# A 16x512x1024 by 1024x768 product with a subtraction: smaller row groups, a pinned order, and a transpose of f16 pairs as 32-bit words

## The chip, the cores and the metric

The kernel runs on one core of one Trainium2 chip. The metric is the device time in microseconds (us) of one execution; three runs of the kernel before gave 228.85, 230.29 and 231.27 us.

## The reference

```python
def setup_inputs():
    batch, m, k, n = 16, 512, 1024, 768
    return {
        "x": np.random.randn(batch, m, k).astype(np.float32),
        "weight": np.random.randn(k, n).astype(np.float32),
        "sub_value": np.random.randn(batch, m, n).astype(np.float32),
    }

def reference(x, weight, sub_value):
    return (np.matmul(x, weight) - sub_value).astype(np.float32)
```

Flattened, x is 8192 rows of 1024, and out and sub_value are 8192 rows of 768, all f32.

## The kernel before

The 8192 rows of x are cut into 64 "m tiles" of 128 rows. Four m tiles make a group (`SUP = 4`), and one DMA moves a whole group of x (2 MB), of sub_value or of out (1.5 MB each), with four neighbouring rows of memory on one partition. There are 16 groups.

Each m tile goes through five steps. ScalarE casts its x rows from f32 to f16 (L104, `do_cast`). TensorE transposes the 128x1024 f16 tile in eight blocks of 128x128, each a weight load of the x block and a matmul with the f16 identity (L112, `do_transpose`), into one PSUM tile. ScalarE copies the transposed tile to SBUF (L117, `xt_tile`). TensorE then multiplies: for the output columns 0 to 511 and again for 512 to 767 it runs over the eight k tiles (L127, `do_matmul`), so 8 matmuls of 512 columns and 8 of 256, each with its own weight load of an `xt_tile` block. VectorE subtracts sub_value from PSUM into `out_tile` (L136), and after the fourth m tile one DMA stores the group (L143).

The weight is read at the start in eight pieces of 128 k rows (L88) through a staging pool of two buffers, and VectorE casts each piece to f16 (L89). All DMAs are issued by SyncE (SP) on one queue. A scheduler orders the instructions of each engine; the source is written with casts 9 m tiles ahead and transposes 6 m tiles ahead of the matmuls (`C_AHEAD`, `T_AHEAD`), and the pools hold 4 x groups, 3 sub groups, 2 out groups, 8 `xt_tile`, 4 PSUM tiles for transposes and 2 for products.

Of the kernel before, what the change touches and what calls it, by code (L numbers as in the profile page):

```python
# [1 line left out]

# [5 lines left out]

P = 128
F32 = mybir.dt.float32  # L10
F16 = mybir.dt.float16


@with_exitstack
def kernel(
    ctx: ExitStack,
    tc: tile.TileContext,
    x: bass.AP,
    weight: bass.AP,
    sub_value: bass.AP,  # L20
    out: bass.AP,
):
    nc = tc.nc

    x_flat = x.flatten_outer_dims()
    sub_flat = sub_value.flatten_outer_dims()
    out_flat = out.flatten_outer_dims()

    M_TOT, K = x_flat.shape
    _, N = weight.shape  # L30
    assert M_TOT % P == 0
    assert K % P == 0
    n_mtiles = M_TOT // P
    n_ktiles = K // P

    SUP = 4
    assert n_mtiles % SUP == 0
    n_sup = n_mtiles // SUP

    x_sup_ap = x_flat.rearrange("(s p j) k -> s p j k", p=P, j=SUP)  # L40
    sub_sup_ap = sub_flat.rearrange("(s p j) n -> s p j n", p=P, j=SUP)
    out_sup_ap = out_flat.rearrange("(s p j) n -> s p j n", p=P, j=SUP)

    n_splits = []
    n0 = 0
    while n0 < N:
        w = min(512, N - n0)
        n_splits.append((n0, w))
        n0 += w

    T_AHEAD = 6
    C_AHEAD = 9
    X_AHEAD = 3

    const_pool = ctx.enter_context(tc.tile_pool(name="const", bufs=1))
    w_stage_pool = ctx.enter_context(tc.tile_pool(name="w_stage", bufs=2))
    w_pool = ctx.enter_context(tc.tile_pool(name="w_pool", bufs=1))
    x_pool = ctx.enter_context(tc.tile_pool(name="x_pool", bufs=X_AHEAD + 1))
    x16_pool = ctx.enter_context(tc.tile_pool(name="x16_pool", bufs=6))
    xt_pool = ctx.enter_context(tc.tile_pool(name="xt_pool", bufs=T_AHEAD + 2))  # L60
    sub_pool = ctx.enter_context(tc.tile_pool(name="sub_pool", bufs=3))
    out_pool = ctx.enter_context(tc.tile_pool(name="out_pool", bufs=2))
    psum_t_pool = ctx.enter_context(tc.tile_pool(name="psum_t", bufs=4, space=bass.MemoryType.PSUM))
    psum_o_pool = ctx.enter_context(tc.tile_pool(name="psum_o", bufs=2, space=bass.MemoryType.PSUM))

    identity = const_pool.tile([P, P], F16)
    make_identity(nc, identity)

    w_sb = w_pool.tile([P, n_ktiles, N], F16)

    x_tiles: dict[int, bass.AP] = {}

    def load_x_sup(s):
        t = x_pool.tile([P, SUP, K], F32, tag="x", name="x_tile")
        x_tiles[s] = t
        nc.sync.dma_start(out=t, in_=x_sup_ap[s])  # L76

    sub_tiles: dict[int, bass.AP] = {}

    def load_sub_sup(s):  # L80
        t = sub_pool.tile([P, SUP, N], F32, tag="sub", name="sub_tile")
        sub_tiles[s] = t
        nc.sync.dma_start(out=t, in_=sub_sup_ap[s])

    load_x_sup(0)
    for kt in range(n_ktiles):
        w_stage = w_stage_pool.tile([P, N], F32, name="w_stage")
        nc.sync.dma_start(out=w_stage, in_=weight[kt * P : (kt + 1) * P, :])  # L88
        nc.vector.tensor_copy(out=w_sb[:, kt], in_=w_stage)  # L89
    for s in range(1, X_AHEAD + 1):  # L90
        if s < n_sup:
            load_x_sup(s)
    load_sub_sup(0)
    if n_sup > 1:
        load_sub_sup(1)

    x16_tiles: dict[int, bass.AP] = {}
    xt_tiles: dict[int, bass.AP] = {}

    def do_cast(mi):  # L100
        s, j = divmod(mi, SUP)
        t = x16_pool.tile([P, K], F16, name="x16_tile")
        x16_tiles[mi] = t
        nc.scalar.copy(out=t, in_=x_tiles[s][:, j])  # L104

    def do_transpose(mi):
        x16_tile = x16_tiles.pop(mi)
        xt_tile = xt_pool.tile([P, n_ktiles, P], F16, name="xt_tile")
        xt_tiles[mi] = xt_tile
        psum_t = psum_t_pool.tile([P, n_ktiles, P], F16, name="psum_t")  # L110
        for kt in range(n_ktiles):
            nc.tensor.transpose(  # L112
                psum_t[:, kt, :],
                x16_tile[:, kt * P : (kt + 1) * P],
                identity,
            )
        nc.scalar.copy(out=xt_tile, in_=psum_t)  # L117

    out_tiles: dict[int, bass.AP] = {}

    def do_matmul(mi):
        s, j = divmod(mi, SUP)
        xt_tile = xt_tiles.pop(mi)
        psum_o = psum_o_pool.tile([P, N], F32, name="psum_o")
        for n0, nw in n_splits:
            for kt in range(n_ktiles):
                nc.tensor.matmul(  # L127
                    psum_o[:, n0 : n0 + nw],
                    xt_tile[:, kt, :],
                    w_sb[:, kt, n0 : n0 + nw],  # L130
                    start=(kt == 0),
                    stop=(kt == n_ktiles - 1),
                )
        if j == 0:
            out_tiles[s] = out_pool.tile([P, SUP, N], F32, name="out_tile")
        nc.vector.tensor_tensor(  # L136
            out=out_tiles[s][:, j],
            in0=psum_o,
            in1=sub_tiles[s][:, j],
            op=mybir.AluOpType.subtract,  # L140
        )
        if j == SUP - 1:
            nc.sync.dma_start(out=out_sup_ap[s], in_=out_tiles.pop(s))  # L143

    for mi in range(min(C_AHEAD, n_mtiles)):
        do_cast(mi)
    for mi in range(min(T_AHEAD, n_mtiles)):
        do_transpose(mi)

    for mi in range(n_mtiles):  # L150
        s, j = divmod(mi, SUP)
        if j == 0:
            if s + X_AHEAD + 1 < n_sup:
                load_x_sup(s + X_AHEAD + 1)
            if s + 2 < n_sup:
                load_sub_sup(s + 2)
        if mi + C_AHEAD < n_mtiles:
            do_cast(mi + C_AHEAD)
        if mi + T_AHEAD < n_mtiles:
            do_transpose(mi + T_AHEAD)  # L160
        do_matmul(mi)


# [1 line left out]
_INS = ['x', 'weight', 'sub_value']  # L165
_OUTS = [((16, 512, 768), 'float32')]


# [23 lines left out]
```

## Time and profile before

| what | value |
|---|---|
| median of the runs | 230.29 us (228.85 to 231.27) |
| profiled execution: its span, first to last instruction (the page gives no other time of it) | 229.0 us |
| TensorE matmul busy | 203.4 us, 89% |
| TensorE weight load busy | 132.6 us, 58% |
| ScalarE busy | 124.0 us, 54% |
| VectorE busy | 65.8 us, 29% |
| moved by DMA | 87.26 MB, mean 381 GB/s |
| granted TensorE clock, mean | 0.961 |

Busy time is the sum of the recorded durations on an engine; TensorE overlaps neighbouring matmuls, so a recorded duration (219 ns for a transpose) is longer than the distance from one start to the next. The median of the timed runs lies 1.3 us above the profiled span.

### The profile page before, as it was taken

The numbers are of one execution on the slowest core, as the hardware profiler recorded it, in microseconds if no ns is written. First come the engines' busy times: TensorE is split into PE (matmuls) and PEld (weight loads), VectorE is DVE, ScalarE is ACT, GpSimd is POOL, SyncE is SP. The second block draws the span as 40 slices with busy tenths as digits, with TensorE's granted clock in tenths as the row PEclk, the third lists the DMA queues.
The fourth block names the chain that finished last, engine by engine and source line by source line (L and its number), as shares of the span: only waits on it lengthen the run. The fifth ranks groups of instructions, "written<-read, shape, count | busy, mean of one in ns | idle before, by whom it ended". The sixth has DMA issues, their size and how long they took to land.

```text
span 229.0 us, 3465 instructions
## 1 busy us (share of the span) xinstructions
PE 203.4 (89%) x1536; PEld 132.6 (58%) x1536; DVE 65.8 (29%) x72; ACT 124.0 (54%) x129; POOL 0.7 (0%) x6
## 2 busy tenths in 40 slices
PE   0259559999999999999999999999999999999970
PEld 0236325666666676666757576667575766666540
DVE  0101113333333331423332413333332413233430
ACT  2499863382583666566583939475656565510000
POOL 1000000000000000000000000000000000000000
PEclk9995967999999999999999999999999999999996
DMA  6999999999999999999999999999999999750606
GB/s 235 421 429 401 427 431 432 419 399 412 352 427 427 439 419 433 425 436 420 430 429 431 423 424 426 431 426 423 429 423 435 424 416 350 305 240 39 271 6 275
DMA packets 8079, 87.26 MB, mean 381 GB/s; under 512 B 896, under 2 KB 896, under 8 KB 1920
## 3 DMA queue, kind: packets, MB, share of 16 engines
q1 hardware_dynamic: 8064, 87.04, 91.1%
q8 instruction: 12, 0.20, 0.3%
q14 instruction: 3, 0.02, 0.0%
HBM read 61.87 MB, written 25.17 MB: 380 GB/s over the span
## 4 chain that ended last, share of the span: by engine, by line
PE 82%; DMA 12%; DVE 1%; ACT 0%; SPq 0%; issue 0%
PE psum_o L127 72%; DMA w_stage<-in_weight_dram 12%; PE psum_t L112 10%; DVE w_sb L89 1%; ACT xt_tile L117 0%; DVE out_tile L136 0%; SPq L88 0%; SPq L76 0%
## 5 line engine op out<-in xcount | busy, mean ns | idle before, releaser
L127 PE MATMUL psum_o<-w_sb,xt_tile 128*128 128x512 f16 (+1 forms) x1024 | 174.7, 330 | 3.6 <-DVE w_sb L89 3.1
L127 PEld LDWEIGHTS <-xt_tile 128*128 128x128 f16 x1024 | 100.1, 99 | 70.3 <-issue 4.6
L117 ACT COPY xt_tile<-psum_t 128x1024 f16<-128x1024 f16 x64 | 63.2, 1016 | 68.9 <-PE psum_t L112 37.6
L136 DVE TENSOR_TENSOR out_tile<-psum_o,sub_tile 128x768 f32<-128x768 f32 x64 | 61.3, 958 | 129.4 <-PE psum_o L127 126.2
L104 ACT CAST x_tile<-x_tile 128x1024 f16<-128x1024 f32 x64 | 63.5, 1053 | 8.8 <-DMA x_tile<-in_x_dram 8.8
L112 PE MATMUL psum_t<-identity,x_tile 128*128 128x128 f16 x512 | 37.4, 230 | 15.1 <-ACT x_tile L104 14.6
L112 PEld LDWEIGHTS <-x_tile 128*128 128x128 f16 x512 | 33.7, 104 | 19.0 <-ACT x_tile L104 16.1
L89 DVE CAST w_sb<-w_stage 128x768 f16<-128x768 f32 x8 | 4.5, 560 | 27.9 <-DMA w_stage<-in_weight_dram 27.9
L104 ACT ACT_TABLE_LOAD x1 | 1.3, 1283 | 0.7 <-PEq L176 0.7
masks.py:199 POOL TENSOR_SCALAR_AFFINE_SELECT identity<-identity 128x128 f16<-128x128 f16 x1 | 0.3, 294 | 0.1
masks.py:197 POOL MEMSET identity<- 128x128 f16 x1 | 0.2, 205 | 0.3 <-POOLq L176 0.3
L176 POOL MEMSET const-bfloat16-1.0<- 128x1 bf16 x1 | 0.1, 102 | 0.0
L176 POOL MEMSET const-uint8-127<- 128x1 uint8 x1 | 0.1, 102 | 0.0
L176 POOL MEMSET const-float32-0.0<- 128x1 f32 x1 | 0.1, 99 | 0.2 <-issue 0.2
L176 POOL MEMSET const-float32-1.0<- 128x1 f32 x1 | 0.1, 99 | 0.0
## 6 DMA issues: line engine op xcount, KB each, us to landing
x_tile<-in_x_dram SPq DMA_DIRECT2D x16, 2048.0 KB, 14.6
sub_tile<-in_sub_value_dram SPq DMA_DIRECT2D x16, 1536.0 KB, 17.8
out_dram<-out_tile SPq DMA_DIRECT2D x16, 1536.0 KB, 10.1
w_stage<-in_weight_dram SPq DMA_DIRECT2D x8, 384.0 KB, 6.3
```

The lines of the kernel that those rows point to most:

```text
L89: nc.vector.tensor_copy(out=w_sb[:, kt], in_=w_stage)
L104: nc.scalar.copy(out=t, in_=x_tiles[s][:, j])
L112: nc.tensor.transpose(psum_t[:, kt, :], x16_tile[:, kt * P : (kt + 1) * P], identity,)
L117: nc.scalar.copy(out=xt_tile, in_=psum_t)
L127: nc.tensor.matmul(psum_o[:, n0 : n0 + nw], xt_tile[:, kt, :], w_sb[:, kt, n0 : n0 + nw], start=(kt == 0), stop=(kt == n_ktiles - 1),)
L136: nc.vector.tensor_tensor(out=out_tiles[s][:, j], in0=psum_o, in1=sub_tiles[s][:, j], op=mybir.AluOpType.subtract,)
L176: nc = _bacc.Bacc("TRN2", target_bir_lowering=False, num_devices=1)
```

## The change

The kernel is rewritten around the same arithmetic in f16 with f32 accumulation.

- Groups are of two m tiles (`J = 2`), 32 of them. x moves in DMAs of 1 MB, sub_value and out in DMAs of 0.75 MB. The first x group is loaded in two halves.
- The weight comes in four pieces of 256 k rows (L73), each with a staging buffer of its own. In a piece, partition p holds the rows 2p and 2p+1, so the k index is split as (piece c, partition p, parity r).
- The f16 x tile is viewed as 128x512 words of 32 bits, each holding two neighbouring k. TensorE transposes four blocks of 128x128 words (L110) with an f32 identity. In the transposed tile the two k of a word stay side by side, so the stationary operand of a matmul (L127, L129) is taken with a step of two f16.
- The output is halved in 2 x 384 columns, one PSUM bank each, in place of 512 and 256; the product tiles in PSUM are three, the transpose tiles two.
- The result is written over the loaded sub_value tile (L142, `so_tile`), and the store (L89) goes out of it. There are 11 such tiles.
- Every instruction is kept in program order. TensorE issues a transpose of the m tile two ahead (`TA`) after every four matmuls; the cast runs four m tiles ahead. SP issues at the start of group g the load of x group g+4, of sub group g+2, and then the store of group g-2, and the last two stores behind the loop.

```diff
+J = 2
+D = 6
+TA = 2
+CA = 2
...
-    x_pool = ctx.enter_context(tc.tile_pool(name="x_pool", bufs=X_AHEAD + 1))
-    x16_pool = ctx.enter_context(tc.tile_pool(name="x16_pool", bufs=6))
-    xt_pool = ctx.enter_context(tc.tile_pool(name="xt_pool", bufs=T_AHEAD + 2))
-    sub_pool = ctx.enter_context(tc.tile_pool(name="sub_pool", bufs=3))
-    out_pool = ctx.enter_context(tc.tile_pool(name="out_pool", bufs=2))
-    psum_t_pool = ctx.enter_context(tc.tile_pool(name="psum_t", bufs=4, space=bass.MemoryType.PSUM))
-    psum_o_pool = ctx.enter_context(tc.tile_pool(name="psum_o", bufs=2, space=bass.MemoryType.PSUM))
-
-    identity = const_pool.tile([P, P], F16)
-    make_identity(nc, identity)
...
+    w_stage_pool = ctx.enter_context(tc.tile_pool(name="w_stage", bufs=n_c))
+    w_pool = ctx.enter_context(tc.tile_pool(name="w_pool", bufs=1))
+    x_pool = ctx.enter_context(tc.tile_pool(name="x_pool", bufs=6))
+    x16_pool = ctx.enter_context(tc.tile_pool(name="x16_pool", bufs=4))
+    xt_pool = ctx.enter_context(tc.tile_pool(name="xt_pool", bufs=4))
+    so_pool = ctx.enter_context(tc.tile_pool(name="so_pool", bufs=11))
+    psum_t_pool = ctx.enter_context(tc.tile_pool(name="psum_t", bufs=2, space=bass.MemoryType.PSUM))
+    psum_o_pool = ctx.enter_context(tc.tile_pool(name="psum_o", bufs=3, space=bass.MemoryType.PSUM))
+
+    ident = const_pool.tile([P, P], F32)
+    make_identity(nc, ident)
...
+    def load_w(c):
+        st = w_stage_pool.tile([P, 2, N], F32, name="w_stage")
+        keep(nc.sync.dma_start(out=st, in_=w_c[c]))
+        keep(nc.vector.tensor_copy(out=w_sb[:, c], in_=st))
...
+        def one(c):
+            def f():
+                if c == 0:
+                    start()
+                keep(nc.tensor.transpose(
+                    ps_t[mi].bitcast(F32)[:, c * P : (c + 1) * P],
+                    x16_t[mi].bitcast(F32)[:, c * P : (c + 1) * P],
+                    ident,
+                ))
+                if c == n_c - 1:
+                    fin()
+            return f
...
+                c, r = divmod(kt, 2)
+                lhsT = xt_t[mi][:, 2 * P * c + r : 2 * P * (c + 1) : 2]
+                for h in range(2):
+                    keep(nc.tensor.matmul(
+                        po_t[mi][:, h, :NS],
+                        lhsT,
+                        w_sb[:, c, r, h * NS : (h + 1) * NS],
+                        start=(kt == 0),
+                        stop=(kt == n_kt - 1),
+                    ))
...
+    load_x(0, 0)
+    load_w(0)
+    load_x(0, 1)
+    for c in range(1, n_c):
+        load_w(c)
+    load_x(1)
+    load_x(2)
+    load_sub(0)
+    load_x(3)
+    load_sub(1)
...
+        if g + 4 < n_g:
+            load_x(g + 4)
+        if g + 2 < n_g:
+            load_sub(g + 2)
+        if g - (D - 4) >= 0:
+            store(g - (D - 4))
...
+        for kt in range(n_kt):
+            mm[kt]()
+            if tr and kt % per == per - 1:
+                tr.pop(0)()
+        if mi + CA + TA < n_mt:
+            cast(mi + CA + TA)
+        finish(mi)
+    for g in range(n_g - (D - 4), n_g):
+        store(g)
```

In the middle of the program TensorE's row before passes from the last product of one m tile to a batch of transposes, each with a weight load row of its own (the names are those of the tiles; `x_tile` is the cast f16 tile here):

```order
L127 LDWEIGHTS xt_tile
L127 MATMUL psum_o<-w_sb,xt_tile 128x256
L112 LDWEIGHTS x_tile
L112 MATMUL psum_t<-identity,x_tile 128x128
L112 LDWEIGHTS x_tile
L112 MATMUL psum_t<-identity,x_tile 128x128
```

At the same place of the program after, a transpose stands alone between the products:

```order
L129 LDWEIGHTS xt_tile
L129 MATMUL psum_o<-w_sb,xt_tile 128x384
L110 MATMUL psum_t<-ident,x_tile 128x128
L129 LDWEIGHTS xt_tile
L129 MATMUL psum_o<-w_sb,xt_tile 128x384
```

What moved: the transposes are no longer in batches but one behind every four products, and the transpose of 32-bit words has no weight load row of its own; the one instruction loads its words itself.

SP's row at the start of the program before puts whole x groups between the pieces of the weight:

```order
L76 DMA x_tile<-in_x_dram 128x4096
L88 DMA w_stage<-in_weight_dram 128x768 x2
L76 DMA x_tile<-in_x_dram 128x4096
L88 DMA w_stage<-in_weight_dram 128x768 x2
L76 DMA x_tile<-in_x_dram 128x4096
L88 DMA w_stage<-in_weight_dram 128x768 x2
L76 DMA x_tile<-in_x_dram 128x4096
L88 DMA w_stage<-in_weight_dram 128x768 x2
L83 DMA sub_tile<-in_sub_value_dram 128x3072 x2
```

And after:

```order
L82 DMA x_tile<-in_x_dram 128x1024
L73 DMA w_stage<-in_weight_dram 128x1536
L82 DMA x_tile<-in_x_dram 128x1024
L73 DMA w_stage<-in_weight_dram 128x1536 x3
L80 DMA x_tile<-in_x_dram 128x2048 x2
L86 DMA so_tile<-in_sub_value_dram 128x1536
L80 DMA x_tile<-in_x_dram 128x2048
L86 DMA so_tile<-in_sub_value_dram 128x1536
```

What moved: one x group of two m tiles and the whole weight, 4.2 MB, now stand ahead of everything else in the queue, where 8 MB of x stood before the last pieces of the weight.

More of the change, by code (lines that the diff above doesn't have):

```diff
@@ L23 @@
     nc = tc.nc
+    keep = tc.keep_in_program_order
     x_flat = x.flatten_outer_dims()
@@ L30 @@
     _, N = weight.shape
[L31 to L49, printed above, removed]
@@ L64 @@
-    psum_o_pool = ctx.enter_context(tc.tile_pool(name="psum_o", bufs=2, space=bass.MemoryType.PSUM))
-    identity = const_pool.tile([P, P], F16)
-    make_identity(nc, identity)
[L69 to L101, printed above, removed]
-        t = x16_pool.tile([P, K], F16, name="x16_tile")
-        x16_tiles[mi] = t
-        nc.scalar.copy(out=t, in_=x_tiles[s][:, j])
@@ L106, in do_transpose @@
[L106 to L161, printed above, removed]
+    x_pool = ctx.enter_context(tc.tile_pool(name="x_pool", bufs=6))
@@ new lines @@
+    x16_pool = ctx.enter_context(tc.tile_pool(name="x16_pool", bufs=4))
[5 more added lines that the diff above has]
+    make_identity(nc, ident)
+    w_sb = w_pool.tile([P, n_c, 2, N], F16)
@@ new lines, with load_x @@
+    x_t = {}
+    so_t = {}
+    x16_t = {}
+    xt_t = {}
+    ps_t = {}
+    po_t = {}
+    def load_w(c):
+        st = w_stage_pool.tile([P, 2, N], F32, name="w_stage")
+        keep(nc.sync.dma_start(out=st, in_=w_c[c]))
+        keep(nc.vector.tensor_copy(out=w_sb[:, c], in_=st))
+    def load_x(g, js=None):
+        if g not in x_t:
+            x_t[g] = x_pool.tile([P, J, K], F32, name="x_tile")
+        if js is None:
+            keep(nc.sync.dma_start(out=x_t[g], in_=x_g[g]))
+        else:
+            keep(nc.sync.dma_start(out=x_t[g][:, js], in_=x_g[g][:, js]))
@@ new lines, in load_sub, with store, cast, transposes @@
+    def load_sub(g):
+        so_t[g] = so_pool.tile([P, J, N], F32, name="so_tile")
+        keep(nc.sync.dma_start(out=so_t[g], in_=sub_g[g]))
+    def store(g):
+        keep(nc.sync.dma_start(out=out_g[g], in_=so_t.pop(g)))
+    def cast(mi):
+        g, j = divmod(mi, J)
+        t = x16_pool.tile([P, K], F16, name="x16_tile")
+        x16_t[mi] = t
+        keep(nc.scalar.copy(out=t, in_=x_t[g][:, j]))
+    def transposes(mi):
+        def start():
+            ps_t[mi] = psum_t_pool.tile([P, K], F16, name="psum_t")
+        def fin():
+            xt = xt_pool.tile([P, K], F16, name="xt_tile")
+            xt_t[mi] = xt
+            keep(nc.scalar.copy(out=xt, in_=ps_t.pop(mi)))
+            x16_t.pop(mi)
+        def one(c):
[10 more added lines that the diff above has]
+            return f
+        return [one(c) for c in range(n_c)]
@@ new lines, in matmuls, with one, f @@
+    def matmuls(mi):
+        def one(kt):
+            def f():
+                if kt == 0:
+                    po_t[mi] = psum_o_pool.tile([P, 2, 512], F32, name="psum_o")
+                c, r = divmod(kt, 2)
[8 more added lines that the diff above has]
+                    ))
+            return f
+        return [one(kt) for kt in range(n_kt)]
@@ new lines, in finish, with transfers @@
+    def finish(mi):
+        g, j = divmod(mi, J)
+        o = so_t[g][:, j].rearrange("p (h n) -> p h n", h=2)
+        keep(nc.vector.tensor_tensor(
+            out=o, in0=po_t.pop(mi)[:, :, :NS], in1=o, op=mybir.AluOpType.subtract
+        ))
+    load_x(0, 0)
[8 more added lines that the diff above has]
+    load_sub(1)
+    def transfers(g):
+        if g + 4 < n_g:
[4 more added lines that the diff above has]
+            store(g - (D - 4))
@@ new lines @@
+    for mi in range(TA):
+        cast(mi)
+        for f in transposes(mi):
+            f()
+    for mi in range(TA, CA + TA):
+        cast(mi)
+    for mi in range(n_mt):
+        if mi % J == 0:
+            transfers(mi // J)
+        mm = matmuls(mi)
+        tr = transposes(mi + TA) if mi + TA < n_mt else []
+        per = max(1, n_kt // len(tr)) if tr else 1
+        for kt in range(n_kt):
[5 more added lines that the diff above has]
+        finish(mi)
```

13 lines of the change are left out of this document (9 added, 4 removed).

## The prediction

> **What bounds the kernel now.** I read the page first, for who is busy when, then the chain that ended last in order of time, then the windows for the rate of the transfers.
>
> ```profile
> span 229.0 us, 3465 instructions
> ...
> PE 82%; DMA 12%; DVE 1%; ACT 0%; SPq 0%; issue 0%
> ```
>
> The chain is TensorE for 82% of the span and a transfer for 12%. In order of time it shows where each of the two stands:
>
> ```profile
> 1.64 9.14 DMA w_stage<-in_weight_dram
> ...
> 25.13 6.69 DMA w_stage<-in_weight_dram
> ...
> 54.20 0.45 PE psum_t L112 x8
> 54.64 2.60 PE psum_o L127 x16
> ...
> 194.34 1.79 PE psum_t L112 x32
> 196.13 26.02 PE psum_o L127 x160
> ...
> 222.17 0.96 DVE out_tile L136
> ```
>
> Until 31.8 us the chain runs through the weight's pieces; from 32.5 us on it is TensorE without a hole. One m tile costs 0.45 us for eight transposes (0.45/8 = 56 ns each) and 2.60 us for sixteen matmuls (162 ns on average). That is 3.05 us, and 64 x 3.05 = 195 us. Now the transfers, in three stretches:
>
> ```profile
> core 0: us, PE busy (x) PEld busy (x) DVE busy (x) ACT busy (x) POOL busy (x), PEclk, DMA share, GB/s
> 0.00:5.00 5.00, 0.00 (x0) 0.00 (x0) 0.00 (x0) 1.28 (x1) 0.70 (x6) 1.00 0.64 206
> 5.00:185.00 180.00, 166.28 (x1286) 109.56 (x1287) 52.35 (x58) 113.07 (x118) 0.00 (x0) 0.96 1.01 423
> 185.00:229.00 44.00, 37.13 (x252) 23.02 (x249) 13.41 (x14) 9.66 (x10) 0.00 (x0) 0.95 0.57 231
> 10.00:30.00 20.00, 13.23 (x108) 9.29 (x109) 3.21 (x6) 18.10 (x20) 0.00 (x0) 0.83 1.01 419
> ...
> DMA packets 8079, 87.26 MB, mean 381 GB/s; under 512 B 896, under 2 KB 896, under 8 KB 1920
> ```
>
> From 5 to 185 us the DMA engines are full (share 1.01) at 423 GB/s. So **two resources are full at once**: TensorE needs 195 us and starts 32 us late, the transfers need 87.26 MB / 423 GB/s = 206 us and start at once. TensorE ends last only because of its late start. In the last 44 us the transfers run at half rate.
>
> **The change part by part.** First the *floor by transfers*, which no edit lowers: the bytes stay. The first 5 us moved 1.03 MB, worth 2.4 us at 423 GB/s, so the queue loses 2.6 us at the start. 2.6 + 206.3 = 208.9 us. The end costs a little more, as the answers for the store's line and for SP's waits show:
>
> ```profile
> L143 SPq DMA_DIRECT2D out_dram<-out_tile x16: 332/344/348, 44.8 to 223.2; - x16
> ...
> DMA to landing us min/median/max: 5.0/10.1/12.6
> ```
>
> ```profile
> SPq L187 <- DMA out_dram<-out_tile: 4.4, 1, 4.4
> ```
>
> The quickest store took 5.0 us for 1.57 MB, which at 423 GB/s is 3.7 us; 1.3 us is latency, part of it hidden in a full queue. The last store was issued at 223.2 us and, with SP's last wait of 4.4 us behind its issue of 0.3, landed at about 228; the span ended at 229.0, some 0.8 us later. I take 1.5 us for both: 210.4. Smaller pieces (8 and 6 KB per partition instead of 16 and 12) could cost something: the stretch from 10 to 30 us carried the weight in rows of 3 KB between the x groups and still ran at 419, 1% under 423. So between 0 and 1.5% of 206, or 0 to 3 us; I take 1. **Floor 211.5 us.**
>
> Does the queue stay full? SP keeps several transfers ahead; with the order of group g (x of g+4, sub of g+2, store of g-2), a store waits for a group that TensorE left a whole group ago, and behind it stand only loads that are needed three or four groups later. The last five stores follow the last sub load; each group of them is finished while the ones before are being written, so TensorE's end stays ahead of the queue if TensorE is the faster one.
>
> Second, *TensorE's own time*. Its start: x group 0 (1.05 MB), the weight (3.15) and x group 1 (1.05) are 5.24 MB. That is 2.6 + 5.24/0.423 = 15.0, with a microsecond to land 16 us. The pinned order needs group 1 before the fifth matmul, since the first transpose of m tile 2 stands there; its cast takes a microsecond more by the row below, so TensorE passes that point at 17.1 us, not at 32.5. In front of it lies only work that fits beside the loading.
>
> ```profile
> L127 PE MATMUL psum_o<-w_sb,xt_tile 128*128 128x512 f16 x512 | 124.1, 383 | 3.6 <-DVE w_sb L89 3.1 <-ACT xt_tile L117 0.3
> L127 PEld LDWEIGHTS <-xt_tile 128*128 128x128 f16 x1024 | 100.1, 99 | 70.3 <-issue 4.6 <-ACT xt_tile L117 1.1
> L127 PE MATMUL psum_o<-w_sb,xt_tile 128*128 128x256 f16 x512 | 68.1, 277 | 0.0
> L104 ACT CAST x_tile<-x_tile 128x1024 f16<-128x1024 f32 x64 | 63.5, 1053 | 8.8 <-DMA x_tile<-in_x_dram 8.8
> L117 ACT COPY xt_tile<-psum_t 128x1024 f16<-128x1024 f16 x64 | 63.2, 1016 | 68.9 <-PE psum_t L112 37.6 <-PE psum_o L127 30.9
> L136 DVE TENSOR_TENSOR out_tile<-psum_o,sub_tile 128x768 f32<-128x768 f32 x64 | 61.3, 958 | 129.4 <-PE psum_o L127 126.2 <-DMA sub_tile<-in_sub_value_dram 3.2
> L112 PE MATMUL psum_t<-identity,x_tile 128*128 128x128 f16 x512 | 37.4, 230 | 15.1 <-ACT x_tile L104 14.6 <-ACT xt_tile L117 0.5
> L112 PEld LDWEIGHTS <-x_tile 128*128 128x128 f16 x512 | 33.7, 104 | 19.0 <-ACT x_tile L104 16.1 <-issue 1.7
> ```
>
> Sixteen matmuls of 384 columns stream the same 6144 columns as eight of 512 and eight of 256, so 2.60 us again. A weight load of 99 ns lies beside a matmul of 162 ns. Its step of two f16 is not in the trace; a load would have to grow by 63 ns before it shows, so I take 0, and 63 ns beyond that as the upper end would cost 64 x 16 x 63 ns = 65 us of TensorE, a case that I count among the slow ones below.
>
> The transposes: eight of 56 ns go, four of t come. The trace has no transpose of 32-bit words. From below t is 56 ns, a transpose of the same 128 columns. From above, the nearest rows give 56 + 99 = 155 ns if the words' load, which is now inside the instruction, isn't hidden by the matmul before; 4 x 56 = 224 ns if a word of four bytes passes in four trips; and 323 ns for both. I take 56 to 90: the same count of columns and rows moves, and four matmuls stand ahead of each transpose to hide its load.
>
> Sum of TensorE: 17.1, the rest of m tile 0 at 12 x 0.162 = 1.95, 63 m tiles x 2.60 = 163.8, 248 transposes at t, then the subtraction 0.96, the store's issue 0.3, 0.79 MB / 423 GB/s = 1.9, its latency 1.3 and the end 0.8: **188.1 us + 248 t**. At t = 56 ns that is 202, under the floor. It meets the floor of 211.5 at t = 94 ns, and the span of before, 229.0, at t = 165 ns. So four transposes of up to 94 ns are free, and every further 10 ns cost 2.5 us.
>
> ScalarE keeps 1.05 + 1.02 = 2.07 us per m tile and VectorE 0.96, both under the 206.3/64 = 3.2 us that the transfers leave per m tile. TensorE will then wait about a tenth of the time; from 10 to 30 us it was busy for two thirds and the granted clock fell to 0.83, while at full work it stands at 1.00 or close by. Waits of a few tenths of a us between m tiles I cost at nothing, since a slower clock would fill them first. The in-place subtraction reads and writes as much as before, at the same 958 ns: 0. The store of a group holds its tile longer, but eleven tiles are a lead of nine groups. Four casts of the weight, each twice 560 ns, lie beside the loading.
>
> Span 211.5 us; the median of the runs stood 1.3 us over the profiled span of before, so I forecast **213 us** for the median, against 230.3.
>
> Two rules of the Trainium skill bear on t. Its page "TensorE: Matmul & The Clock Gate", section "Weight-path perf modes — Fast Weight Load (FWL) and DoubleRow", says that the fast weight load is on for 128 weights only where the type isn't f32. No run shown has an f32 load, so the trace can't say; by the page's P/1.2 = 107 ns for a plain load, an estimate, and no overlap, t would be 56 + 107 = 163 ns and the span 228.5. The same page's table of terms gives the transpose mode as four times faster for f32, which by an estimate would leave one trip in place of four, t = 56 ns and the floor. The page's section "Part 4: PE-mode transpose" has about 275 ns for a transpose in a kernel; this trace's rows disagree, 8 in 0.45 us.
>
> **The rivals.**
>
> *The words' load shows.* The order gives no weight load row for the new transpose; nothing in the trace says whether the engine still loads early. If it all shows, t = 155 ns, TensorE sets the end again, 188.1 + 248 x 0.155 = 226.5, and the time is 228, the edge of no change. Partly hidden, between 94 and 155 ns, it is 213 to 228. The skill's rule on the fast weight load, above, speaks for this rival. For it: the instruction carries its own load, and the two full resources leave room for only 94 ns. Against: the f16 batches load in 104 ns by the recorded mean and still start every 56 ns, so loads run beside other work.
>
> *Slower: a word takes four trips.* The place is each of the 248 transposes inside the stream of products; the price 224 ns each, the span 188.1 + 55.6 = 243.7, the time 245. With the load showing as well, 323 ns, it is 268 and 269.5. It decides from t = 165 ns. For it: twice the bytes per column on the same engine, and nothing in this trace that shows a 32-bit operand at any speed. A stepped weight load that outgrows its matmul would end on the same side. Against: the words are moved, not multiplied.
>
> *The queue doesn't stay full.* SP stands still at a store, or smaller pieces run slower than 419. Each GB/s of the rate is 0.5 us, so at 400 GB/s the span is 223. Against: 423 over 180 us, with the same engine waiting at each store as it does now.
>
> **How the numbers follow.** A change of under 1% (2.3 us) can't be told from none by three runs. The floor within 209 to 216: 0.55. TensorE or a thinner queue between 216 and 228: 0.22. No change, 228 to 232.6: 0.07. Slower, mostly 245 to 270: 0.16. The range takes the first three and their lower edge, 209 to 231, and leaves out the slow case and a little on both sides. Faster by over 1%: 0.77; within 1%: 0.07; slower: 0.16.
>
> **What would show it.** Right: in the middle of the profile a DMA share near 1.0 and over 410 GB/s to the last 10 us, TensorE with short waits for ScalarE's casts, which wait for x transfers, about 2.9 us of work in each 3.2 us; the matmuls under way by 17 us; four transposes in under 0.38 us. Wrong: TensorE without holes and an m tile of over 3.1 us; a transpose of 32-bit words that keeps the next product waiting by over 100 ns; transfers under 400 GB/s; or matmuls of 384 columns more than 170 ns apart.

## The result and the profile after

The changed kernel takes 220.19 us (median of four runs, 219.24 to 220.60) against 230.49 us before: ratio 0.955, 95% interval 0.952 to 0.959. It is faster, by 10.3 us where 17.3 were forecast; the time lies inside the range of 209 to 231, 7.2 us over the forecast of 213. The profiled execution has a span of 217.4 us and a time of 219.24; the other three have spans of 218.1 to 218.8.

The page of the changed kernel, its head and the chain by engine:

```profile
span 217.4 us, 3150 instructions
...
PE 89%; DMA 6%; SPq 1%; ACT 0%; DVE 0%; issue 0%
```

The transfer in the chain shrank from 12% to 6% of the span, and nearly all of the rest is TensorE. So TensorE still sets the end. The chain in order of time begins with the one transfer that is left in it and ends as before:

```profile
4.24 12.42 DMA x_tile<-in_x_dram
16.68 1.05 ACT x_tile L95
...
206.94 5.21 PE psum_o L129 x32
212.18 0.96 DVE so_tile L142
```

x group 1 lands at 16.7 us, is cast, and from 17.8 us TensorE runs without a hole to 212.1 us. The windows show the transfers full beside it to 185 us:

```profile
0.00:5.00 5.00, 0.00 (x0) 0.00 (x0) 0.00 (x0) 1.28 (x1) 0.70 (x6) 1.00 0.60 170
5.00:185.00 180.00, 170.70 (x1105) 118.86 (x1106) 55.52 (x58) 111.77 (x114) 0.00 (x0) 1.00 1.01 423
185.00:217.40 32.40, 27.14 (x177) 18.29 (x175) 9.58 (x10) 13.77 (x14) 0.00 (x0) 0.96 0.76 315
```

(Columns as in the windows of before: busy time of TensorE, its weight loads, VectorE, ScalarE and GpSimd, then granted clock, DMA share and GB/s.) The transfers are full at 423 GB/s as before; in the last 32 us they run at 315 where they ran at 231 in the last 44. Now TensorE's order of time in the middle, start and recorded length in us:

```profile
126.96 0.27 PE L110 MATMUL psum_t<-ident,x_tile 128*128 128x128 f32 x1
127.07 0.81 PE L129 MATMUL psum_o<-w_sb,xt_tile 128*128 128x384 f16 x4
127.72 0.27 PE L110 MATMUL psum_t<-ident,x_tile 128*128 128x128 f32 x1
127.83 0.81 PE L129 MATMUL psum_o<-w_sb,xt_tile 128*128 128x384 f16 x4
128.48 0.27 PE L110 MATMUL psum_t<-ident,x_tile 128*128 128x128 f32 x1
```

One transpose and four matmuls repeat every 0.76 us (126.96, 127.72, 128.48), and the four take 0.65. A transpose of 32-bit words takes 0.109 us of the stream, start to start (the expectations below have it as 108 ns). Four of them are 0.44 us per m tile; eight f16 ones were 0.45. The m tile went from 3.05 to 3.04 us: **the transposes gave back in price what they saved in number**, and the whole gain is that TensorE starts earlier. Its stretch without a hole begins 14.7 us earlier than before (17.8 against 32.5 us) and lasts 4.6 us longer (194.3 against 189.7), because TensorE before, while it waited for the weight, had already transposed twelve m tiles and run 14 matmuls, while the changed kernel had two m tiles and four matmuls behind it; so 10 us of the 14.7 are left at its end.

### The profile page after: what moved, and what is told of

Same layout as the page of the kernel before. It is cut to its first block, busy times and chain, and to the rows that moved or that the text cites. A ratio compares the mean times of both kernels' runs of the same rounds, so it can differ in the third digit from the quotient of the medians.

```text
span 217.4 us, 3150 instructions
## 1 busy us (share of the span) xinstructions
PE 197.8 (91%) x1280; PEld 137.1 (63%) x1280; DVE 65.1 (30%) x68; ACT 126.8 (58%) x129; POOL 0.7 (0%) x6
## 4 chain that ended last, share of the span: by engine, by line
PE 89%; DMA 6%; SPq 1%; ACT 0%; DVE 0%; issue 0%
PE psum_o L129 77%; PE psum_t L110 13%; DMA x_tile<-in_x_dram 6%; SPq L73 1%; ACT x_tile L95 0%; DVE so_tile L142 0%; SPq L82 0%
## 5 line engine op out<-in xcount | busy, mean ns | idle before, releaser
L129 PE MATMUL psum_o<-w_sb,xt_tile 128*128 128x384 f16 x1024 | 195.6, 328 | 0.0
L129 PEld LDWEIGHTS <-xt_tile 128*128 128x128 f16 x1024 | 100.9, 99 | 43.1 <-issue 1.0
L104 ACT COPY xt_tile<-psum_t 128x1024 f16<-128x1024 f16 x64 | 64.8, 1012 | 72.4 <-PE psum_t L110 72.4
L142 DVE TENSOR_TENSOR so_tile<-psum_o,so_tile 128x768 f32<-128x768 f32 x64 | 61.3, 957 | 136.7 <-PE psum_o L129 136.7
L110 PE MATMUL psum_t<-ident,x_tile 128*128 128x128 f32 x256 | 70.2, 279 | 14.3 <-ACT x_tile L95 14.3
L95 ACT CAST x_tile<-x_tile 128x1024 f16<-128x1024 f32 x64 | 67.0, 1048 | 8.1 <-DMA x_tile<-in_x_dram 8.0
L110 PEld LDWEIGHTS psum_t<-ident,x_tile 128*128 128x128 f32 x256 | 36.5, 144 | 31.5 <-ACT x_tile L95 9.0
L74 DVE CAST w_sb<-w_stage 128x1536 f16<-128x1536 f32 x4 | 3.8, 960 | 11.3 <-DMA w_stage<-in_weight_dram 11.3
## 6 DMA issues: line engine op xcount, KB each, us to landing
x_tile<-in_x_dram SPq DMA_DIRECT2D x31, 1024.0 KB, 16.6
so_tile<-in_sub_value_dram SPq DMA_DIRECT2D x32, 768.0 KB, 16.6
```

Of the source, the lines that this page charges most:

```text
L74: keep(nc.vector.tensor_copy(out=w_sb[:, c], in_=st))
L95: keep(nc.scalar.copy(out=t, in_=x_t[g][:, j]))
L104: keep(nc.scalar.copy(out=xt, in_=ps_t.pop(mi)))
L110: keep(nc.tensor.transpose(ps_t[mi].bitcast(F32)[:, c * P : (c + 1) * P], x16_t[mi].bitcast(F32)[:, c * P : (c + 1) * P], ident,))
L129: keep(nc.tensor.matmul(po_t[mi][:, h, :NS], lhsT, w_sb[:, c, r, h * NS : (h + 1) * NS], start=(kt == 0), stop=(kt == n_kt - 1),))
L142: keep(nc.vector.tensor_tensor(out=o, in0=po_t.pop(mi)[:, :, :NS], in1=o, op=mybir.AluOpType.subtract))
```

## The experiments

Two theories stood against each other. A: the gain is the start of the queue alone, the word transpose costs 108 ns because its columns pass at half the rate of f16 ones, and what is missing to the forecast is TensorE's rest above a floor by transfers at 211.5 us. B: the word transpose, or the order that goes with it, carries part of the gain, its load is what costs, or there is no such floor. Ratios are to the kernel before on the same chip, with their 95% intervals. The changed kernel run once more beside the later ones:

> The changed kernel once more, on the chip of the other two, to be set beside them: span 217 to 219, time 219 to 221, ratio 0.95 to 0.96, by every theory.

It measured 219.82 us, ratio 0.956 (0.952 to 0.961), span 217.6.

### Eight f16 transposes in the changed kernel

```diff
-    w_c = weight.rearrange("(c p r) n -> c p r n", p=P, r=2)
+    w_c = weight.rearrange("(c r p) n -> c p r n", p=P, r=2)
...
-    ident = const_pool.tile([P, P], F32)
+    ident = const_pool.tile([P, P], F16)
...
-                    ps_t[mi].bitcast(F32)[:, c * P : (c + 1) * P],
-                    x16_t[mi].bitcast(F32)[:, c * P : (c + 1) * P],
+                    ps_t[mi][:, c * P : (c + 1) * P],
+                    x16_t[mi][:, c * P : (c + 1) * P],
...
-                if c == n_c - 1:
+                if c == n_kt - 1:
...
-        return [one(c) for c in range(n_c)]
+        return [one(c) for c in range(n_kt)]
...
-                lhsT = xt_t[mi][:, 2 * P * c + r : 2 * P * (c + 1) : 2]
+                lhsT = xt_t[mi][:, kt * P : (kt + 1) * P]
```

> The changed kernel with the one part on the transpose undone: eight f16 transposes of 128x128 per m tile with an f16 identity (one behind every two matmuls), k rows in plain order, all else as changed. Theory A (the gain is the start alone; the word transpose costs 108 ns in the stream, so four of them equal eight of 56 ns): an m tile goes from 3.035 to 2.60 + 8 x 0.056 = 3.05 us, the span from 217.4 to about 218.4, the time about 221, ratio to before 0.955 to 0.965. Theory B (the word transpose carries part of the gain, because single f16 transposes between matmuls show their load of about 100 ns): 2.60 + 8 x 0.104 = 3.43 us, span about 242, slower than before.

221.42 us, ratio 0.961 (0.957 to 0.965), span 219.1. Its order of time, one transpose behind two matmuls:

```profile
120.00 0.22 PE L110 MATMUL psum_t<-ident,x_tile 128*128 128x128 f16 x1
120.06 0.49 PE L129 MATMUL psum_o<-w_sb,xt_tile 128*128 128x384 f16 x2
120.38 0.22 PE L110 MATMUL psum_t<-ident,x_tile 128*128 128x128 f16 x1
```

A transpose and two matmuls take 0.38 us, so a single f16 transpose is about 0.056 us even alone among matmuls. Theory A holds: the words are worth about 1 us of the 10, and the intervals of the two ratios overlap (0.952 to 0.959 with words). The weight loads with a step of two f16 cost nothing, since four matmuls take 0.65 us with them (above) and two take 0.325 without.

### What a word transpose pays for

The load of 64 columns of words instead of 128, twice as many instructions, all 128 identity columns streamed in each; the upper half of each transposed tile is set to zero once, and ScalarE copies the lower 64 partitions alone:

```diff
...
-                    ps_t[mi].bitcast(F32)[:, c * P : (c + 1) * P],
-                    x16_t[mi].bitcast(F32)[:, c * P : (c + 1) * P],
+                    ps_t[mi].bitcast(F32)[: P // 2, c2 * P : (c2 + 1) * P],
+                    x16_t[mi].bitcast(F32)[:, c2 * P + a : c2 * P + a + P // 2],
...
```

> The changed kernel with each word transpose cut in two that load 64 columns of words and stream all 128 columns of the identity; the upper 64 partitions of the transposed tile stay zero, so the output is another one. Eight instructions per m tile. Theory A (a 32-bit transpose costs 108 ns because its 128 columns stream at half the rate): 8 x 0.108 = 0.86 us per m tile, 3.46 in all, span about 244. Theory B (it costs 108 ns because its load of 128 columns shows): 64 columns load in half the time, 8 x 0.054 = 0.43, span as changed, 217.

247.61 us in one run, span 245.8. Its groups:

```profile
L117 PE MATMUL psum_t<-ident,x_tile 128*64 128x128 f32 x512 | 139.9, 279 | 13.3 <-ACT x_tile L101 13.3
...
L117 PEld LDWEIGHTS psum_t<-ident,x_tile 128*64 128x64 f32 x512 | 58.1, 114 | 47.4 <-ACT x_tile L101 8.1 <-issue 7.3
```

The recorded load fell from 144 to 114 ns, the transpose's recorded 279 ns did not move, and neither did its place in the stream:

```profile
120.45 0.27 PE L117 MATMUL psum_t<-ident,x_tile 128*64 128x128 f32 x1
120.56 0.49 PE L136 MATMUL psum_o<-w_sb,xt_tile 128*128 128x384 f16 x2
120.88 0.27 PE L117 MATMUL psum_t<-ident,x_tile 128*64 128x128 f32 x1
```

0.435 us less two matmuls at 0.1625 is 0.11 us. Half the columns loaded, the same price: theory B falls, the load is not what costs. The price fits theory A, 128 columns at half the rate of f16 (109 ns against 56), but a fixed price for each transpose of words would read the same here. The counter-test, which could tell the two apart, loads all 128 columns from the lower 64 partitions and streams 64 columns:

```diff
...
-                    ps_t[mi].bitcast(F32)[:, c * P : (c + 1) * P],
-                    x16_t[mi].bitcast(F32)[:, c * P : (c + 1) * P],
-                    ident,
+                    ps_t[mi].bitcast(F32)[:, c2 * P + a : c2 * P + a + P // 2],
+                    x16_t[mi].bitcast(F32)[: P // 2, c2 * P : (c2 + 1) * P],
+                    ident[: P // 2, : P // 2],
...
```

> The changed kernel with each word transpose cut in two that load all 128 columns of words of the lower 64 partitions and stream 64 columns of the identity; rows 64 to 127 of an m tile are replaced by rows 0 to 63 in it, so the output is another one. Eight instructions per m tile. Theory A (streaming at half the rate): 8 x 0.054 = 0.43 us, span as changed, 217. Theory B (the load of 128 columns shows): 8 x 0.108 = 0.86 us, span about 244.

551.99 us, which neither theory gave. The transpose and two matmuls now take 1.05 us:

```profile
120.63 0.37 PE L111 MATMUL psum_t<-ident,x_tile 64*128 64x64 f32 x1
120.93 0.82 PE L130 MATMUL psum_o<-w_sb,xt_tile 128*128 128x384 f16 x2
121.68 0.37 PE L111 MATMUL psum_t<-ident,x_tile 64*128 64x64 f32 x1
```

The next matmul begins 0.30 us after the transpose, and the two matmuls, which do what they did, take 0.75 us in place of 0.325. What sets the small transpose apart from its neighbours, 64 rows and 64 streamed columns among matmuls on 128 rows, costs more than everything that was to be measured, so this run says nothing on A or B; that the change of the row size is the cause was not tested by itself. So the load is ruled out, and the price by the column remains the likely reading, not a shown one. The third test of the load puts the four transposes in one batch, where no matmul stands between them:

```diff
-            if tr and kt % per == per - 1:
-                tr.pop(0)()
+        for f in tr:
+            f()
```

> The changed kernel with the four word transposes of an m tile in one batch behind its sixteen matmuls. Theory A (the price is streaming; the load lies beside the work ahead of it): 108 ns each, span 217 to 218. Theory B (the load of about 144 ns is hidden only by a matmul ahead of it): three of four show it, 4 transposes take about 0.6 us, an m tile 3.2, span about 228.

217.54 us, ratio 0.945 (0.942 to 0.949), span 215.7:

```profile
122.59 0.60 PE L110 MATMUL psum_t<-ident,x_tile 128*128 128x128 f32 x4
123.03 2.76 PE L129 MATMUL psum_o<-w_sb,xt_tile 128*128 128x384 f16 x16
125.63 0.60 PE L110 MATMUL psum_t<-ident,x_tile 128*128 128x128 f32 x4
```

Four in 0.44 us, 0.11 each, so nothing of the load shows in a batch either; A holds on the price. The 1.7 us of span that it is shorter than the changed kernel were not expected. They come from the start: with no transpose of m tile 2 among them, the matmuls of m tile 0 are done at about 16 us and not at 21.5. The section on the start of the changed kernel takes this up.

### The floor by transfers

Two of four word transposes are left out, and ScalarE copies half of each transposed tile:

```diff
-            keep(nc.scalar.copy(out=xt, in_=ps_t.pop(mi)))
+            keep(nc.scalar.copy(out=xt[:, : K // 2], in_=ps_t.pop(mi)[:, : K // 2]))
...
-        return [one(c) for c in range(n_c)]
+        return [one(c) for c in range(n_c // 2)]
...
-                lhsT = xt_t[mi][:, 2 * P * c + r : 2 * P * (c + 1) : 2]
+                lhsT = xt_t[mi][:, 2 * P * (c // 2) + r : 2 * P * (c // 2 + 1) : 2]
```

> The changed kernel with two of the four word transposes per m tile left out; the products use the first half of k twice, so the output is another one, with the same matmuls and transfers. Theory A (TensorE sets the end of the changed kernel; the floor by transfers lies at a span of 211.5): TensorE alone would end its span at 217.4 - 124 x 0.108 = 204, so the floor shows: 211 to 213, time 213 to 215, TensorE with waits for casts. Theory B (transfers and TensorE end together already, the floor is at 217): span 216 to 218, no change. Theory C (no floor near): 204.

214.41 us, ratio 0.930 (0.927 to 0.933), span 212.5, where TensorE alone would have ended at 204. Its waits show who holds it:

```profile
DVE so_tile L142 <- DMA so_tile<-in_sub_value_dram: 69.9, 18, 4.4
ACT xt_tile L104 <- PE psum_t L110: 64.2, 54, 2.5
DVE so_tile L142 <- PE psum_o L129: 53.4, 29, 2.8
ACT x_tile L95 <- DMA x_tile<-in_x_dram: 34.0, 14, 5.7
```

VectorE and ScalarE now wait for transfers for 104 us in all (69.9 + 34.0); in the changed kernel ScalarE waited 8.0 us for x and VectorE not at all for sub_value. The transfers run at 423 GB/s to 205 us, with TensorE waiting. The floor of the prediction, 211.5, is there: 212.5.

### The start of the changed kernel

The transposes of m tiles 2 and 3 behind the matmuls of m tiles 0 and 1, not among them:

```diff
-            if tr and kt % per == per - 1:
+            if tr and mi > 1 and kt % per == per - 1:
                 tr.pop(0)()
+        if mi <= 1:
+            for f in tr:
+                f()
```

> The changed kernel with the transposes of m tiles 2 and 3 behind the matmuls of m tiles 0 and 1 and not among them. Theory A (the pinned order makes the first m tile wait for x group 1): m tile 0 is done with the last weight piece at about 15.5 us and its successor's transposes at 18.3 instead of 21.6: span about 214, time about 217. Theory B (the slow clock or the weight itself sets the start): no change, 217.

216.03 us, ratio 0.939 (0.936 to 0.941), 4.2 us under the changed kernel's 220.19 where about 3 were expected. Four of the five executions have spans of 214.2 to 214.3 us, as theory A has it. The profiled one was the longest, with a span of 215.9 and a time of 217.65. In it m tile 0 is done with the last weight piece, as expected, but m tile 1's sixteen matmuls then took 4.3 us (18.3 to 22.6) and not 2.6; the granted clock reads 0.50 from 18.3 to 21.7 us, and 3.4 us at half the clock are the 1.7 us lost. The changed kernel has the same slowness in m tile 0:

```profile
17.78 0.47 PE L110 MATMUL psum_t<-ident,x_tile 128*128 128x128 f32 x1 [5.74 <-ACT x_tile L95]
18.05 1.49 PE L129 MATMUL psum_o<-w_sb,xt_tile 128*128 128x384 f16 x4
19.32 0.42 PE L110 MATMUL psum_t<-ident,x_tile 128*128 128x128 f32 x1
19.54 1.30 PE L129 MATMUL psum_o<-w_sb,xt_tile 128*128 128x384 f16 x4
20.67 0.27 PE L110 MATMUL psum_t<-ident,x_tile 128*128 128x128 f32 x1
20.78 0.81 PE L129 MATMUL psum_o<-w_sb,xt_tile 128*128 128x384 f16 x4
```

After an idle stretch of 5.7 us the first matmuls take about 0.32 us each, twice the later 0.16, and it ends three microseconds on. The windows give the granted clock as 1.00 there, but the trace has no entry of the clock before 20.5 us, where the matmuls come to full speed. Where there are entries, the slowness goes with the clock: 0.50 in the run above, and 0.50 from 17.6 to 20.9 us in the run with batches, where the matmuls start 0.32 us apart too. What lowers the clock was not tested by itself; in those two runs TensorE had stood idle for 1.8 us, not 5.7.

A larger change of the start loads x for three m tiles among the weight pieces and multiplies the three together as the pieces arrive:

```diff
...
+    mm0 = [matmuls(mi) for mi in range(H0)]
+    for c in range(n_c):
+        if c == n_c - 1:
+            cast(H0)
+            for f in transposes(H0):
+                f()
...
+        for mi in range(H0):
+            for r in range(2):
+                mm0[mi][2 * c + r]()
...
```

(Not shown: the order of the first transfers, six f16 and transposed x tiles instead of four, and the passage to the steady loop.)

> The changed kernel with another start: x for three m tiles is loaded among the first weight pieces, and while the pieces arrive TensorE runs every arrived piece for the m tiles 0, 1 and 2 at once; from m tile 3 on as changed. Theory A (late start of TensorE is what still costs): three m tiles done at about 19 to 20 us instead of 27.7, TensorE's end 8 us earlier at 209, under the floor by transfers of 211.5: span 211 to 213, time 213 to 215, ratio to before 0.925 to 0.935. Theory B (transfers are the end already): span 216 to 218, no change.

217.57 us, ratio 0.944 (0.941 to 0.947), span 215.9: neither 212 nor 217. The x loads put ahead delayed the weight, whose second piece was cast at 12.3 us instead of 10.4 and whose last at 17.3 instead of 14.2, but TensorE didn't wait for it: the matmuls began at 13.75 us, behind the transposes of three m tiles, and ran without a gap. Up to about 18 us they start 0.32 us apart, the slowness named above; the first 36 took 8.0 us where 36 at 0.1625 are 5.9. So the matmuls of m tile 3 began at about 24 us, four later than expected, and a further 1.2 us were lost in a wait for a cast before 29.8 us. A simpler one keeps the queue as it is and multiplies only m tiles 0 and 1 together, with the transposes of 2 and 3 behind both:

```diff
...
+    transfers(0)
+    mm0 = [matmuls(mi) for mi in range(TA)]
+    for c in range(n_c):
+        for mi in range(TA):
+            for r in range(2):
+                mm0[mi][2 * c + r]()
...
+    for mi in range(TA, 2 * TA):
+        for f in transposes(mi):
+            f()
...
-    for mi in range(n_mt):
+    for mi in range(TA, n_mt):
...
```

> The changed kernel with m tiles 0 and 1 multiplied together, each piece of the weight for both as it arrives, then the transposes of m tiles 2 and 3; everything later as changed, same queue. Theory A (what is left above the floor is TensorE's start): two m tiles and four transposed by about 19.5 us in place of 24.6, TensorE would end 4 us or more earlier, the floor by transfers shows: span 212 to 213.5, time 214 to 215.5, ratio 0.93 to 0.937. Theory B (no gain beyond moving the first transposes, 215.9): 215.5 to 216.5.

215.58 us, ratio 0.937 (0.933 to 0.940), span 213.7, beside 219.82 for the changed kernel on the same chip: the fastest of the runs with the full output, 1.2 us of span over the floor that was measured. The span lies between what the two theories expected, just over A's 212 to 213.5. Most of the gain is that of moving the first transposes: against the 214.2 to 214.3 us of four executions there, multiplying the two m tiles together is worth another half microsecond. TensorE is idle for one microsecond of the stretch from 20 to 40 us and full after it.

### The start of the kernel before

Four staging buffers for the weight instead of two, nothing else:

```diff
-    w_stage_pool = ctx.enter_context(tc.tile_pool(name="w_stage", bufs=2))
+    w_stage_pool = ctx.enter_context(tc.tile_pool(name="w_stage", bufs=4))
```

> The kernel before with four staging buffers for the weight in place of two, nothing else; the weight then stands in the queue behind one x group, 5.2 MB in all, and not between four of them. Theory A (the start is the gain): the last weight piece lands at 16 us in place of 31.8, TensorE runs without a hole from about 17 us: 17 + 64 x 3.05 + 6.9 = 219 us span, about 220 us, ratio 0.95 to 0.965, the same as the whole change. Theory B (smaller groups, pinned order or word transposes carry the gain): 225 to 230.

232.99 us, ratio 1.011 (1.007 to 1.014): slower by 1%, so theory A's 220 falls, and it lies over B's 225 to 230 too. The last weight piece was cast at 18.6 us, as meant, but the chain now waits elsewhere:

```profile
13.36 10.13 DMA x_tile<-in_x_dram
23.51 3.88 ACT x_tile L104 x4
...
37.65 1.98 PE psum_t L112 x16
39.62 16.17 PE psum_o L127 x96
```

```profile
DVE out_tile L136 <- DMA sub_tile<-in_sub_value_dram: 19.4, 1, 19.4
```

The first sub_value group stood behind four x groups of 2 MB and landed at 38.5 us; with two product tiles in PSUM TensorE could not multiply a third m tile, and the scheduler had put the transposes of later groups ahead of it. Its first subtraction and the last of these transposes ended at the same time, 39.5 and 39.6 us, so both held the third m tile back. In the kernel before, with its late weight, VectorE waited only 3.2 us for the sub group. So next the sub group came forward too, with the four staging buffers kept:

```diff
...
+    load_sub_sup(0)
     for s in range(1, X_AHEAD + 1):
         if s < n_sup:
             load_x_sup(s)
-    load_sub_sup(0)
```

> The kernel before with four staging buffers for the weight and the first sub_value group ahead of x groups 1 to 3 in the queue. Theory A (the start of before is set by the order of the whole queue: with the weight early, the two product tiles then waited for the first sub group, which lands at 38 us): sub group 0 lands at about 20 us, the products of the first group run from 17 us, x group 1 lands at 25: TensorE about 8 us earlier than before, span 220 to 223, ratio 0.96 to 0.975. Theory B (groups of 2 MB are too large for any order to help): 227 to 231.

227.63 us, ratio 0.989 (0.984 to 0.995), far from theory A's 0.96 to 0.975 and at the lower edge of theory B's 227 to 231. Now the second x group is waited for 10.9 us and the second sub group 11.3 us: in groups of 2 MB whatever is put ahead pushes something else back. The last run takes the group size and the queue's order together, with the changed kernel's shorter leads, and leaves the transposes, the tiles of results and the scheduler's freedom as they were:

```diff
-    SUP = 4
+    SUP = 2
...
-    T_AHEAD = 6
-    C_AHEAD = 9
+    T_AHEAD = 2
+    C_AHEAD = 4
...
-    w_stage_pool = ctx.enter_context(tc.tile_pool(name="w_stage", bufs=2))
+    w_stage_pool = ctx.enter_context(tc.tile_pool(name="w_stage", bufs=8))
...
-    for s in range(1, X_AHEAD + 1):
-        if s < n_sup:
-            load_x_sup(s)
+    load_x_sup(1)
+    load_x_sup(2)
     load_sub_sup(0)
-    if n_sup > 1:
-        load_sub_sup(1)
+    load_x_sup(3)
+    load_sub_sup(1)
```

(The pools of x, sub and out tiles are 6, 6 and 4 of the smaller tiles.)

> The kernel before with groups of two m tiles, eight staging buffers for the weight, the queue's first transfers in the order of the changed kernel, and its leads (transposes 2, casts 4 m tiles ahead); still eight f16 transposes per m tile, matmuls of 512 and 256, results in tiles of their own, the order left to the scheduler. Theory A (group size and queue order at the start carry the gain): two m tiles multiplied and six transposed at about 23 us, then 62 x 2.60 + 58 x 0.45 = 187 us, end 5 to 6 us: span 215 to 218, time 216 to 220, as the whole change. Theory B (the pinned order, the word transposes or the in-place result carry part of it): 222 or more.

218.30 us, ratio 0.947 (0.944 to 0.951), span 216.5. Its windows:

```profile
20.00:40.00 20.00, 18.75 (x134) 11.60 (x135) 6.61 (x7) 13.30 (x14) 0.00 (x0) 0.91 1.01 418
40.00:180.00 140.00, 140.00 (x1105) 92.39 (x1103) 43.33 (x46) 87.77 (x93) 0.00 (x0) 1.00 1.01 423
```

With the f16 transposes, the old split of matmuls and results in tiles of their own, the kernel before is as fast as the changed one, a little faster even. The trace shows a likely reason: with the order left to the scheduler the first two m tiles are multiplied by 16.6 us, where the changed kernel, with its pinned order, is done with the first at about 21.5. So neither the word transposes, the split in 384 columns, the in-place result nor the pinned order is needed for the gain. What carries it is the bundle of this run: smaller groups, the queue's first transfers in another order, more buffers and shorter leads. The weight's buffers alone don't do it, nor with the sub group beside them. How the rest divides between group size and leads was not tested: groups of 2 MB with the short leads would show it, and in the run before this one ScalarE's casts and copies, which the leads place, are 23% of the chain up to 70 us.

## Why the prediction was right or wrong

The direction and the bound came out, the place in the range did not. The forecast was that the floor by transfers sets the end, at a span of 211.5 us, with a chance of 0.55; TensorE sets it, at 217.4. The time of 220.19 us lies in the band from 216 to 228, which had a chance of 0.22 and stood for a load that shows or a thinner queue. Neither came: the time fell into this band by another cause, and that is luck, apart from the sum below, which holds for any price of a transpose. Of the 5.9 us of span over the floor, 3.6 are the word transpose's 109 ns in place of 94 at most, and 2.3 are the start and the stream.

- **Two resources full at once, TensorE last because of its late start**: right. The rate of 423 GB/s from 5 to 185 us is the same after. With less work for TensorE the span goes to 212.5, with an earlier start to 213.7.
- **The floor of 211.5 us**: right within 1 us, shown at 212.5 by leaving transposes out. In part that is two errors against each other: the rate did not change, so the 1 us for smaller pieces was not needed, and without it the sum is 210.4. The first 5 us moved 0.88 MB (175 GB/s) in that run and not 1.03, which is 0.4 us; the rest, 1.7 us, was not followed up.
- **The queue stays full**: right, 423 GB/s to 200 us; the rival of a thinner queue did not come.
- **TensorE's sum, 188.1 us + 248 t**: right in form. With the measured t of 109 ns it gives 215.1; the span was 217.4. Of the 2.3 us, 0.7 are x group 1 (17.8 us, not 17.1), 1.4 the rest of m tile 0, which took 3.8 us and not 1.95 + 4 x 0.109 = 2.4 because of the slow first matmuls, and 0.2 the long stream. The slow matmuls were put at nothing, though the rows of the kernel before that the prediction shows have a granted clock of 0.83 from 10 to 30 us. The tail behind the last matmul, 5.3 us, was as summed.
- **"I take 56 to 90" for t**: this is the step that failed. t measured 109 ns, over the 94 ns at which TensorE meets the floor, so TensorE sets the end and the forecast of 213 became 217.4 + 1.8 = 219.2 in the profiled run. The reason given for the low value, the same count of columns and rows, does not hold: the count is the same, and the transpose takes twice as long. That the other reason, four matmuls ahead that hide the load, is right is shown by the runs on the load. The bound from above by a load that shows, 155 ns, enclosed the value by a mechanism that did not occur. One of the signs named for a wrong forecast came, a word transpose that keeps the next product waiting by over 100 ns, and half of another, TensorE without holes, though with an m tile of 3.04 us and not over 3.1. The sign of four transposes in under 0.38 us did not come, they took 0.44.
- **The rule of the Trainium skill on the fast weight load** ("TensorE: Matmul & The Clock Gate", "Weight-path perf modes"): the load of words is longer in the record, 144 ns against 104, which agrees in direction, but it stays hidden, alone and in a batch, and t is not the 163 ns that followed from it. The factor of four for f32 in the transpose mode, from the same page's "Terms", was worked out in the prediction to t = 56 ns; t is twice that, and no run here has an f32 matmul outside the transposes to test the factor itself. The prediction also set the 275 ns of the Trainium skill's page ("Part 4: PE-mode transpose"), a duration, beside the distance between starts, 8 in 0.45 us; its like are the recorded durations here, 219 to 230 ns for f16 and 273 to 279 ns for words.
- **Eight f16 transposes as what is saved**: so the saving of the change's most visible part was 64 x (8 x 0.056 - 4 x 0.109) = 0.8 us, and the run with f16 transposes, 1.2 to 1.6 us slower, roughly agrees.
- **The stepped weight loads and the matmuls of 384 columns at no cost, the in-place result at no cost**: right, 0.65 us for four matmuls, and 957 ns for a subtraction.
- **The slow rival**: it did not come; the point from which it decides, 165 ns, was not reached.

## What to carry to other kernels

When a page shows two resources full at once, sum each of them with its own start and end, and count what a saving on one is worth only down to the other's floor. Fewer instructions on wider words are no saving until the price of the wide form is measured in the stream: put the break-even (here 94 ns) beside the bounds, and where the bounds lie on both sides of it, say that the forecast hangs on that one number. A late start can be several waits in a row behind one another; taking the first away can make the kernel slower, so the queue's first transfers are to be ordered by when each is needed, in pieces small enough that putting one ahead doesn't push back the next. When a profiled execution is the longest of its kernel's runs, compare the times of all runs before reading a difference from its span.

## What the runs showed of the hardware

- A transpose of 128x128 words of 32 bits takes 109 ns of TensorE's stream, an f16 one 56; halving the columns loaded does not change it (0.11 us).
- A transpose on 64 rows with 64 streamed columns among matmuls on 128 rows costs far more than its recorded 0.37 us lets expect: 1.05 us for it and two matmuls, against 0.435 with the full row size (one run each).
- After 1.8 to 5.7 us without work TensorE's first matmuls started 0.32 us apart, twice the later 0.16, for some 3 us. Where the trace has entries of the clock there, it reads 0.50; in the changed kernel the first entry stands at 20.5 us, where the slowness ends.
- Transfers of 0.75 to 1 MB in pieces of 6 and 8 KB per partition ran at 423 GB/s, as those of 1.5 to 2 MB in 12 and 16 KB did.
